# A streaming skewness kernel: eight pooled load buffers against a hand-synchronised ring of two blocks, a loop for the transposes, and part of the row sums on GpSimd

## Chip, cores, metric

One core of one Trainium2 chip. The metric is the device time of one execution in microseconds (us), taken as the median of several executions. A profiled execution also has a span, from the first to the last recorded instruction, which is about 2 us shorter. Each execution has a state: "slow" is more than 1.5% above the fastest execution of the same kernel.

## The reference

```python
x: (1024, 8192) float32                      # setup: standard normal numbers
mean = np.mean(x, axis=-1, keepdims=True)
std  = np.std(x, axis=-1, keepdims=True)
z    = (x - mean) / (std + 1e-8)
return np.mean(z ** 3, axis=-1).astype(np.float32)      # (1024,)
```

The kernels need three sums of each row, of x, of x² and of x³, and close the third moment from them with a few small operations. So 33.55 MB are read once and nearly nothing is written.

## The kernel before

The rows lie as 8 blocks of 128 partitions x 8192 columns. A block is loaded in units (2 to 8 of them), and a unit is cut into slices. ScalarE (ACT) squares a slice and sums x²; VectorE (DVE) multiplies the square by x and sums x³ (the "cube"); TensorE (PE) sums x by transposing all 128x128 tiles of a block into one PSUM tile, which accumulates; ACT copies that tile, and one matrix product with a column of 1/8192 gives the means. GpSimd (POOL) only does small closing operations.

```python
S1_ACT = {(0, 0): 1024, (1, 0): 1024, (2, 0): 1024}   # ACT sums x of 1024 columns of three units
X_BUFS = 8                                            # eight buffers for units, in a pool
SQ_BUFS = 4
...
for k, (w, n_slices) in enumerate(widths):
    last_unit = b == L and k == len(widths) - 1
    xt = xpool.tile([P, w], FP, tag="x", name=f"x_{b}_{k}")
    loads.append(nc.sync.dma_start(out=xt, in_=xv[b, :, c0 : c0 + w]))
    ...
    for s, e in _slices(w, n_slices):
        if last_unit:
            sq = psum1.tile([P, e - s], FP, tag="sqps", name="sqps")     # only here in PSUM
        else:
            sq = sqpool.tile([P, e - s], FP, tag="sq", name=f"sq_{b}_{k}_{s}")
        act(out=sq, in_=xt[:, s:e], func=AF.Square, scale=s_scale, accum_out=s2u[:, j : j + 1])
        cube = ...
        v.scalar_tensor_tensor(out=cube, in0=sq, scalar=1.0, in1=xt[:, s:e],
                               op0=ALU.mult, op1=ALU.mult, accum_out=s3u[:, j : j + 1])
        j += 1
    ...                                               # the ACT sum of S1_ACT
    for c in range((w - w_act) // P):
        nc.tensor.matmul(out=tp, lhsT=xt[:, c * P : (c + 1) * P], rhs=ident,
                         start=(k == 0 and c == 0), stop=(c0 == C and c == n - 1),
                         is_transpose=True)
    for fn in todo.pop((b, k), ()):                   # closings of earlier blocks
        fn()
```

The first six blocks are closed together while the seventh is worked on, the seventh with three GpSimd operations and the rest on ACT while the eighth is worked on, and the eighth at the end. In the final closing the order on each engine is the order of the program.

## Time and profile before

| | before |
|---|---|
| median of 3 executions (range) | 90.77 us (90.76 to 90.84) |
| span of the profiled one, mean granted TensorE clock | 88.8 us, 0.972 |
| first cube starts / last cube ends | 9.96 / 86.13 us |
| tail: from the last cube to the end of the span | 2.7 us |
| sum of the cubes | 73.2 us: 72.3 for 51 in one group of the profile, and the last one, which the profile lists by itself |

The first cube, the last cube and the tail cut the span into an entry, a middle and an end. Two stretches of the time line of the kernel before show the ends of that cut. The columns are start, duration, engine, source line, operation, output<-inputs, shapes, count, and in brackets the idle time of the engine before it and what ended that.

```profile
8.06 1.78 ACT L213 ACTIVATE sq<-x 128x1888 f32<-128x1888 f32 x1 [5.83 <-DMA x<-in_x_dram]
9.96 2.13 DVE L218 SCALAR_TENSOR_TENSOR sq<-sq,x 128x1888 f32<-128x1888 f32 x1 [8.93 <-ACT sq L213]
...
84.50 0.26 ACT L127 COPY tsb<-tp 128x128 f32<-128x128 f32 x1
85.17 0.95 DVE L218 SCALAR_TENSOR_TENSOR cube<-sqps,x 128x768 f32<-128x768 f32 x1
86.36 0.22 DVE L260 SCALAR_TENSOR_TENSOR skew<-sums,t_l,rr_l 128x1 f32<-128x1 f32 x1 [0.22 <-POOL rr_l L259]
```

The first square starts as the first load lands (the landing records: sixteen shares, 7.34 to 7.97 us). At the end the copy of the transposes (84.50) is done before the last cube, so that only one DVE operation and the store come after it. A cube of 1888 columns takes 2.13 us here.

### The profile page before, as it was taken

Reading aid. Unit: us, or ns where it says so; the run is one execution under the profiler, and the core shown is the slowest. Engines: PE = TensorE matmul, PEld = TensorE weight load, DVE = VectorE, ACT = ScalarE, POOL = GpSimd, SP = SyncE. Lnnn points to the kernel's source line nnn. Section 1 sums busy time; section 2 is a strip of 40 time slices with the busy share of each in tenths; the row PEclk is TensorE's granted clock in tenths of the full one; section 3 lists DMA queues with packets and bytes.
Section 4 is the critical chain, followed back from the end, with each engine's and each line's share of the span. In section 5 each row is a group of like instructions: output and inputs, shape, how many; then the busy total and the mean of one; then the engine's idle time right before and its main releaser. Section 6 shows DMA issues by size and latency. Waiting matters only on the chain.

```text
span 88.8 us, 1435 instructions
## 1 busy us (share of the span) xinstructions
PE 64.2 (72%) x504; PEld 58.4 (66%) x504; DVE 73.9 (83%) x110; ACT 74.4 (84%) x137; POOL 13.7 (15%) x18
## 2 busy tenths in 40 slices
PE   0003999492591996989698989497997989897910
PEld 0003999391590995979496889387896868676710
DVE  1000599999799398999999999999999999999980
ACT  6003999699991899999799999499999999999980
POOL 3000000000000000000000000000000079999930
PEclk9999999999999569999999999999999999999996
DMA  4899999999999999999999999999999999997000
GB/s 118 347 420 435 435 413 450 428 420 435 435 420 413 450 413 435 435 420 428 422 424 398 418 425 423 432 420 420 415 410 423 411 406 410 414 412 282 26 0 2
DMA packets 4038, 33.64 MB, mean 379 GB/s; under 512 B 576, under 2 KB 576, under 8 KB 2368
## 3 DMA queue, kind: packets, MB, share of 16 engines
q1 hardware_dynamic: 4032, 33.56, 90.6%
q8 instruction: 4, 0.07, 0.3%
q14 instruction: 2, 0.02, 0.0%
HBM read 33.55 MB, written 0.00 MB: 378 GB/s over the span
## 4 chain that ended last, share of the span: by engine, by line
DMA 55%; DVE 16%; ACT 13%; issue 7%; SPq 4%; POOLq 1%; POOL 0%; ACTq 0%
DMA x<-in_x_dram 55%; DVE sq L218 16%; ACT sq L213 11%; SPq L206 4%; ACT sqps L213 1%; ACT junk L247 1%; POOLq L294 1%; ACT t L190 0%; DVE skew L260 0%; POOL var_l L258 0%; ACT v L187 0%; ACT nm_l L254 0%; ACT tsb L127 0%; ACTq L213 0%; ACT m1sq_l L253 0%
## 5 line engine op out<-in xcount | busy, mean ns | idle before, releaser
L218 DVE SCALAR_TENSOR_TENSOR sq<-sq,x 128x1568 f32<-128x1568 f32 (+20 forms) x51 | 72.3, 1479 | 11.7 <-ACT sq L213 11.5
L213 ACT ACTIVATE sq<-x 128x1568 f32<-128x1568 f32 (+20 forms) x51 | 63.9, 1256 | 11.1 <-DMA x<-in_x_dram 10.5
L231 PE MATMUL tp<-ident,x 128*128 128x128 f32 x488 | 61.9, 286 | 14.5 <-DMA x<-in_x_dram 14.2
L231 PEld LDWEIGHTS tp<-ident,x 128*128 128x128 f32 x488 | 57.0, 148 | 18.2 <-DMA x<-in_x_dram 10.0
L153 POOL TENSOR_TENSOR vara<-m23a,m1sqa 128x6 f32<-128x6 f32 x1 | 2.0, 1975 | 70.3 <-ACT m1sq3a L157 70.3
L213 ACT ACTIVATION_READ_ACCUMULATOR sq<-x 128x1 f32 x51 | 9.5, 187 | 0.0
L130 PEld LDWEIGHTS s1ps<-onesn,tsb 128*128 128x128 f32 x16 | 2.4, 188 | 8.4 <-ACT tsb L127 8.4
L130 PE MATMUL s1ps<-onesn,tsb 128*128 128x1 f32 x16 | 3.1, 260 | 6.5 <-ACT tsb L127 6.5
L218 DVE DVE_READ_ACCUMULATOR sq<-sq,x 128x1 f32 x51 | 4.2, 83 | 0.0
L225 ACT ACTIVATE same<-x 128x1024 f32<-128x1024 f32 x3 | 3.1, 1045 | 0.0
L154 POOL TENSOR_TENSOR rra<-vara,expo 128x6 f32<-128x6 f32 x1 | 2.9, 2874 | 0.1
L127 ACT COPY tsb<-tp 128x128 f32<-128x128 f32 x8 | 2.0, 246 | 0.0
L102 ACT ACT_TABLE_LOAD x1 | 1.3, 1283 | 0.7 <-PEq L283 0.7
L184 POOL TENSOR_TENSOR rr<-var,expo 128x1 f32<-128x1 f32 x1 | 1.4, 1425 | 0.1
L161 POOL TENSOR_TENSOR m23a<-m23a,m1sq3a 128x6 f32<-128x6 f32 x1 | 1.3, 1267 | 0.1
L162 POOL TENSOR_TENSOR skew<-m23a,rra 128x6 f32<-128x6 f32 x1 | 1.2, 1202 | 0.1
L160 POOL TENSOR_TENSOR m1sq3a<-m1sq3a,nm1a 128x6 f32<-128x6 f32 x1 | 1.2, 1200 | 0.1
L183 POOL TENSOR_TENSOR var<-m23m,m1sq 128x1 f32<-128x1 f32 x1 | 1.0, 1043 | 0.0
L218 DVE SCALAR_TENSOR_TENSOR cube<-sqps,x 128x768 f32<-128x768 f32 x1 | 1.0, 955 | 0.0
L196 POOL TENSOR_TENSOR skew<-t,rr 128x1 f32<-128x1 f32 x1 | 0.8, 842 | 0.1
L213 ACT ACTIVATE sqps<-x 128x768 f32<-128x768 f32 x1 | 0.8, 793 | 0.0
L100 DVE MEMSET onesn<- 128x1 f32 x1 | 0.1, 59 | 0.8 <-PEq L283 0.8
(34 smaller groups left out, 7.9 us busy)
## 6 DMA issues: line engine op xcount, KB each, us to landing
x<-in_x_dram SPq DMA_DIRECT2D x8, 2048.0 KB, 23.4
x<-in_x_dram SPq DMA_DIRECT2D x2, 1472.0 KB, 30.2
x<-in_x_dram SPq DMA_DIRECT2D x3, 832.0 KB, 17.9
x<-in_x_dram SPq DMA_DIRECT2D x4, 576.0 KB, 10.6
x<-in_x_dram SPq DMA_DIRECT2D x2, 896.0 KB, 22.9
x<-in_x_dram SPq DMA_DIRECT2D x1, 1728.0 KB, 33.1
x<-in_x_dram SPq DMA_DIRECT2D x1, 1408.0 KB, 25.2
x<-in_x_dram SPq DMA_DIRECT2D x1, 1216.0 KB, 23.2
```

Of the source, the lines that this page charges most:

```text
L102: nc.scalar.activation(out=tiny, in_=onesn, func=AF.Square)
L127: nc.scalar.copy(out=Tsb[b % 2], in_=tps[b])
L130: nc.tensor.matmul(out=s1ps[:, b : b + 1], lhsT=Tsb[b % 2], rhs=onesn, start=True, stop=True)
L153: g.tensor_tensor(out=vara, in0=m2a, in1=m1sqa, op=ALU.subtract)
L154: g.tensor_tensor(out=rra, in0=vara, in1=expo, op=ALU.pow)
L161: g.tensor_tensor(out=m3a, in0=m3a, in1=m1sq3a, op=ALU.add)
L184: g.tensor_tensor(out=mid["rr"], in0=mid["var"], in1=expo[:, 0:1], op=ALU.pow)
L206: loads.append(nc.sync.dma_start(out=xt, in_=xv[b, :, c0 : c0 + w]))
L213: act(out=sq, in_=xt[:, s:e], func=AF.Square, scale=s_scale, accum_out=s2u[:, j : j + 1],)
L218: v.scalar_tensor_tensor(out=cube, in0=sq, scalar=1.0, in1=xt[:, s:e], op0=ALU.mult, op1=ALU.mult, accum_out=s3u[:, j : j + 1],)
L225: act(out=same[:, 0:w_act], in_=xt[:, w - w_act : w], func=AF.Copy, scale=inv_n, accum_out=s1a[:, b : b + 1],)
L231: nc.tensor.matmul(out=tp, lhsT=xt[:, c * P : (c + 1) * P], rhs=ident, start=(k == 0 and c == 0), stop=(c0 == C and c == n - 1), is_transp ...
```

## The change

The intent, as the diff has it: (a) TensorE's instructions run four times as a loop over two blocks, so that its stream is not fetched piece by piece (the trace before has four fetches of 16 KB for 1008 recorded products and weight loads, by division some 250 to a fetch); (b) to get there with 106 transposes for two blocks, GpSimd adds the first 1536 columns of each block to 128 columns, of which TensorE makes one transpose; (c) the pools become a ring of two whole blocks with semaphores set by hand; (d) ACT loses its three sums. The closings move too.

```diff
-S1_ACT = {(0, 0): 1024, (1, 0): 1024, (2, 0): 1024}
 SUB_MAX = 2304
-X_BUFS = 8
-SQ_BUFS = 4
+SQ_BUFS = 5
+S1_POOL = 1536
+RING = 2
 EARLY = 6
+FOLD_PART = 2
+FETCH_SLOT = 0
...
+    ring = sb("ring", RING * C)
+    fold = [sb(f"fold{i}", S1_POOL // 2) for i in range(RING)]
...
+    def first_sum(b):
+        ...
+        f, n = fold[h], S1_POOL // 2
+        tt(("s1p", b), us + free, f, at(b, 0, n), at(b, n, 2 * n), ALU.add)
+        tt(("s1q", b), [("s1p", b)], f[:, 0 : n // 2], f[:, 0 : n // 2], f[:, n // 2 : n], ALU.add)
+        tt(("s1r", b), [("s1q", b)], f[:, 0:P], f[:, 0:P], f[:, P : 2 * P], ALU.add)
+        pr.op("pool", ("s1s", b), [("s1r", b)], lambda: g.tensor_tensor(
+            out=f[:, 0:P], in0=f[:, 0:P], in1=f[:, 2 * P : 3 * P], op=ALU.add
+        ).then_inc(summed, 1), counts=False)
...
+    for u, (b, k, s, e) in enumerate(units):
+        to_pe(u)                                  # ACT tells TensorE that unit u has landed
+        if s < S1_POOL <= e:
+            first_sum(b)
+        ...                                       # squares, cubes, copy of the sums
+        if (b, k) == (F, 1):
+            first_close()                         # six blocks: 6 operations on GpSimd
+        if (b, k) == (L, 2):
+            mid_close()                           # 7th block: 6 operations on GpSimd (3 before)
...
+    for u, (b, k, s, e) in enumerate(units):      # loads: wait for transposes, fold and cubes
+        free = []                                 # of the block two before
+        ...
+        with nc.Fori(0, NB // RING, engines=type(mybir.ALL_ENGINES)([pe_type]),
+                     head_slot={pe_type: FETCH_SLOT}):
+            for h in range(RING):
+                c0 = S1_POOL
+                for i, end in enumerate(PARTS[h]):
+                    tensor.sem_inc(more, -1)._wait_ge(more, 1)
+                    for c in range(c0, end, P):
+                        t = nc.tensor.matmul(out=tp[h], lhsT=at(h, c, c + P), rhs=ident, ...)
+                    ...
+                    if i == FOLD_PART:
+                        tensor.sem_inc(summed, -1)._wait_ge(summed, 1)
+                        nc.tensor.matmul(out=tp[h], lhsT=fold[h][:, 0:P], rhs=ident, ...)
```

The last cube reads its square from SBUF in the changed kernel, as all the others do.

## The prediction

> **What bounds the kernel now.** I read the page of the kernel before first (busy shares, the 40 slices, the queues), then the costliest groups, the waits, the time line of the last 16 us, and last the landing records of the single loads.
>
> ```profile
> PE 64.2 (72%) x504; PEld 58.4 (66%) x504; DVE 73.9 (83%) x110; ACT 74.4 (84%) x137; POOL 13.7 (15%) x18
> ...
> GB/s 118 347 420 435 435 413 450 428 420 435 435 420 413 450 413 435 435 420 428 422 424 398 418 425 423 432 420 420 415 410 423 411 406 410 414 412 282 26 0 2
> ...
> q1 hardware_dynamic: 4032, 33.56, 90.6%
> q8 instruction: 4, 0.07, 0.3%
> ```
>
> The transfers run at 410 to 450 GB/s from slice 3 to slice 36 without a hole: 33.56 MB at about 425 GB/s is 79 us of an 88.8 us span. So loading is the bound, and the rest is about 1.8 us before the first byte and some 6 us after the last (last DVE cube, power, store). Queue q8 is TensorE's instruction fetch: 4 blocks of 16 KB, at 26.9, 47.1, 63.9 and 81.2 us.
>
> ```profile
> L218 DVE SCALAR_TENSOR_TENSOR sq<-sq,x 128x1568 f32<-128x1568 f32 (+20 forms) x51 | 72.3, 1479 | 11.7 <-ACT sq L213 11.5
> L213 ACT ACTIVATE sq<-x 128x1568 f32<-128x1568 f32 (+20 forms) x51 | 63.9, 1256 | 11.1 <-DMA x<-in_x_dram 10.5
> ...
> L153 POOL TENSOR_TENSOR vara<-m23a,m1sqa 128x6 f32<-128x6 f32 x1 | 2.0, 1975 | 70.3 <-ACT m1sq3a L157 70.3
> ```
>
> The second engine is DVE: its 51 cubes take 72.3 us, 9.0 us a block of 8192 columns, against 79/8 = 9.9 us that DMA needs for a block. **DVE has only 0.8 us of slack a block, some 7 us in all.** That is the number on which this case turns.
>
> The time line of the last 16 us shows something else:
>
> ```profile
> 76.81 1.35 DVE L218 SCALAR_TENSOR_TENSOR sq<-sq,x 128x1152 f32<-128x1152 f32 x1
> 77.03 1.20 POOL L160 TENSOR_TENSOR m1sq3a<-m1sq3a,nm1a 128x6 f32<-128x6 f32 x1
> ...
> 78.17 1.35 DVE L218 SCALAR_TENSOR_TENSOR sq<-sq,x 128x1152 f32<-128x1152 f32 x1
> 78.30 1.27 POOL L161 TENSOR_TENSOR m23a<-m23a,m1sq3a 128x6 f32<-128x6 f32 x1
> ...
> 85.48 0.19 POOL L258 TENSOR_TENSOR var_l<-m_l,m1sq_l 128x1 f32<-128x1 f32 x1 [1.19 <-ACT nm_l L254]
> ```
>
> A GpSimd addition of 6 columns takes 1.2 us while a DVE cube runs (77.03 + 1.20 = 78.23, the cube ends at 76.81 + 1.35 = 78.16), and one of a single column only 0.19 us at 85.48, beside the last cube (85.17 to 86.13), the one cube that takes its square from PSUM and so has a single SBUF input. The additions and products of this stage otherwise end 0.05 to 0.07 us after a cube's end: GpSimd waits for DVE. The reverse (DVE waiting for GpSimd) can't be seen here, as 6 columns fit into the 0.08 us between two cubes.
>
> [...]in the landing records each load's sixteen shares come within 0.6 us up to 22 us; from the first fetch on, one of the sixteen comes 1.5 us late for good, from the second another, from the third a third. The last load ends 2.0 us after its first share, not 0.6.
>
> **The change part by part.**
> 1. *TensorE loops.* Its stream of over 1008 instructions becomes 106 transposes (212 load and multiply instructions) plus means and waits[...], run four times. The three fetches inside the loading go. Worth: the spread of the last load falls from 2.0 us to about 1.1 us (two engines also carry a smaller fetch of another engine, the shares at 1.1 and 0.8 us). **About -1.0 us**, if loading stays the bound. [...]its work of 106 x 0.13 us x 4 = 55 us is spread over 75.
> 2. *GpSimd folds 1536 columns a block to 128.* Four additions of 768, 384, 128 and 128 columns = 1408 columns a block, both inputs in SBUF.[...] GpSimd was idle there, so for itself it is free.[...]
> 3. *Ring of two blocks.* 64 KB a partition replace eight buffers of 16 KB. A load waits for cubes, fold and transposes of the block two before. Four loads of 4.9 us go out at the start, the fifth when the first unit is done, some 8 us after it landed, so about 11 us of loads are still queued: no hole by itself. Once DVE lags, the ring makes the loads wait for DVE, and the GB/s of the slices fall.
> 4. *ACT loses three sums of 1024 columns* (3.1 us busy) and gets 27 small semaphore steps. ACT is ahead of DVE afterwards: no effect on the end.
> 5. *Entry.* One more meeting of the engines before the first load: an estimate of +0.3 us, from the 0.4 us that issuing a load takes here.
> 6. *Tail.* From the closing of the first six blocks GpSimd has 6 + 4 + 6 + 2 = 18 operations in order, and gets one at each end of a cube, of which about 12 are left. Some six remain after the last cubes, at 0.2 to 0.5 us; and the last cube now reads its square from SBUF, so the last variance waits for it: **+1 to +2 us**.
>
> Sum with the lock: first square done at 10.1 us (8.06 + 1.78 + 0.3).[...] Before, the span ended 2.7 us after the last cube (86.1 to 88.8), now an estimated 4: span 111, and 1.9 us from span to time as before (90.77 - 88.8): 113. I choose 110, because the hold may be shorter than the whole instruction[...] and some holds fall into waits of DVE in the first two blocks.
>
> **The rivals.**
> - *DVE isn't held up* (the hold is only as long as a short read, or DVE gets its turn between): then loading stays the bound: 90.8 - 1.0 + 0.3 + 1 to 2 = 91 to 92. For it: no cube in the trace before is longer beside a GpSimd operation (1152 columns: 1.35 us each). Against: those read 6 columns. Also for it, as a matter of judgement: a ring, a loop and an unusual fold are effort that one would hardly keep for a loss.
> - *The fetch was the hidden cost and all goes well*, tail included: 89 to 89.8, 1 to 2% faster; over 2% would need 1.8 us, more than the 1.0 us of the spread.
> - *The ring starves DMA*, if a load waits for fold and transposes that come late: +5 us or so without DVE being busier. Against: about 11 us of loads are queued.
> - *Half a hold* (DVE loses half of the GpSimd time)[...].
>
> **Range and chances.** With the lock[...] 107 to 115, with half of it 98 to 103, without it 89 to 93. I give these 65, 18 and 17 in a hundred. Range 97 to 116. Slower by over 2% (above 92.6): 0.84; within 2%: 0.12; faster: 0.04.
>
> **What would show it.** Right: cubes or the gaps between them grow by 3 us a block; DVE busy or waiting for GpSimd to the end;[...] GB/s falling from 430 to about 340 in the middle slices with loads waiting for DVE; queue q8 empty. Wrong: the rate stays at 420 GB/s to slice 36 and DVE's cubes keep their distance of width/0.96 + 0.08 us; or TensorE waits for the fold while DVE is idle (the ring); or a fetch at each loop end.

The sum of this forecast came to 107.1 us for the end of the last cube, so 97.0 from the first cube's start, to 111 us for the span and 113 us for the time, of which 110 was chosen; for the rival of half a hold it came to 100 us. "The lock" in it is an assumption, that a GpSimd addition and a cube with two SBUF operands hold each other up; the trace of the kernel before shows GpSimd's side of it alone (1.20 us for 6 columns beside a cube). The distance of the cubes is taken from that trace: where DVE doesn't wait, they start width x 1.04 ns + 0.08 us after one another (1.27 us for 1152 columns), and each takes width x 1.04 ns + 0.15 us.

## The result

| | before | after | difference |
|---|---|---|---|
| median, 4 executions each | 90.79 us | 117.64 us (116.92 to 118.08) | +26.9 |
| span of the profiled execution | 88.8 | 115.1 | +26.3 |
| first cube starts | 9.96 | 11.46 | +1.5 |
| from the first cube's start to the last cube's end | 76.2 | 94.3 | +18.2 |
| tail | 2.7 | 9.3 | +6.6 |
| sum of the cubes | 73.2 | 94.2 | +21.1 |
| granted clock | 0.972 | 0.866 | |

The changed kernel is correct and slower: the ratio is 1.295 (95% interval 1.288 to 1.302). A ratio is the mean time of one kernel's fast runs over that of the other's of the same rounds, so it is not quite the ratio of the medians. The time lies 1.6 us above the predicted range.

The page of the kernel after, busy times, rate by slice, and TensorE's fetch queue:

```profile
PE 61.7 (54%) x440; PEld 58.2 (51%) x440; DVE 94.8 (82%) x109; ACT 72.0 (63%) x132; POOL 73.5 (64%) x53
...
GB/s 97 387 444 421 433 427 444 421 438 410 444 353 421 376 307 295 362 351 391 181 397 424 422 323 380 310 267 402 379 390 416 156 0 0 0 0 0 3 0 1
...
q8 instruction: 1, 0.02, 0.1%
```

DVE was 83% busy before as well, but now of a longer span: 94.8 us against 73.9. The loads run at the old rate for the first ten slices (a slice is 2.9 us here) and then break off to between 181 and 400 GB/s in places: they no longer set the pace, and the last fifth of the span has no load at all. TensorE fetches one block of instructions (16 KB) where it fetched four. (That queue q8 is TensorE's is borne out by e12, which changes nothing but TensorE's program against e10: the fetch moves from about 4 us, as in e11, to 12.37 us.)

The groups of the kernel after, and the load queue's waits (total, times, longest):

```profile
L232 DVE SCALAR_TENSOR_TENSOR sq<-sq,ring 128x1568 f32<-128x1568 f32 (+21 forms) x52 | 94.2, 1876 | 10.2 <-ACT sq L223 10.2
L238 POOL TENSOR_TENSOR fold<-ring 128x768 f32<-128x768 f32 x8 | 19.7, 2467 | 21.6 <-DMA ring<-in_x_dram 21.6
L248 POOL TENSOR_TENSOR fold<-fold 128x128 f32<-128x128 f32 x8 | 12.6, 1569 | 0.6
```

```profile
SPq L354 <- DVE sq L232: 50.4, 20, 6.2
```

The 10.2 us that DVE waited for ACT lie before its first cube; after it DVE has 0.1 us of gaps in all. All the added time in the middle is therefore **inside** the cubes. GpSimd's additions of 128 columns take 1.6 us on average, nearly as much as one of 768 columns needs alone (1.82 us, below): most of that is waiting. One block of the time line shows how the two engines take turns:

```profile
19.23 2.46 POOL L238 TENSOR_TENSOR fold<-ring 128x768 f32<-128x768 f32 x1 [1.95 <-DMA ring<-in_x_dram]
...
19.94 3.40 DVE L232 SCALAR_TENSOR_TENSOR sq<-sq,ring 128x1568 f32<-128x1568 f32 x1
...
21.78 3.99 POOL L238 TENSOR_TENSOR fold<-fold 128x384 f32<-128x384 f32 x2
...
23.28 2.17 DVE L232 SCALAR_TENSOR_TENSOR sq<-sq,ring 128x1184 f32<-128x1184 f32 x1
...
25.38 1.80 DVE L232 SCALAR_TENSOR_TENSOR sq<-sq,ring 128x1344 f32<-128x1344 f32 x1
25.84 1.66 POOL L248 TENSOR_TENSOR fold<-fold 128x128 f32<-128x128 f32 x1
...
27.11 2.03 DVE L232 SCALAR_TENSOR_TENSOR sq<-sq,ring 128x1568 f32<-128x1568 f32 x1
```

GpSimd starts its 768 columns at 19.23 and has to wait for the cube in progress, which ends at 20.01. It ends at 21.69, 1.68 us after that end; alone it takes 1.82 us. The cube of 1568 columns that wanted to start at 19.94 takes 3.40 us where it takes 1.79 in a quiet place (that its start falls just before the end of the one ahead is nothing special: nearly all cubes of this trace start 0.07 us before it). The next addition then waits behind that cube, and so on: each addition is let in at a cube's end and lengthens the next cube.

| addition | alone | cube beside it | same cube undisturbed | lost by DVE |
|---|---|---|---|---|
| 768 columns | 1.82 us | 1568: 3.40 | 1.79 | 1.61 |
| 384 | 1.00 | 1184: 2.17 | 1.39 | 0.78 |
| 128 | 0.45 | 1344: 1.80 | 1.55 | 0.25 |
| 128 | 0.45 | 1568: 2.03 | 1.79 | 0.24 |

"Alone" is the addition of the first block before any cube (768 and, up to the first cube's start, 384), and for 128 the mean in experiment e3. The sum of the last column is **2.88 us a block**, 2.0 to 2.1 us for every thousand columns that GpSimd adds. Seven blocks lose 20.2 us and the first one, whose 768 columns ran before any cube, about 1.2: 21.4, against 21.1 measured. (The prediction, and the expectation of e1 with its 21.9, left the last cube out of the sum of the kernel before.) All cubes of the changed kernel read two SBUF operands.

The entry of the kernel after:

```profile
9.48 1.78 ACT L223 ACTIVATE sq<-ring 128x1888 f32<-128x1888 f32 x1 [7.08 <-issue]
```

The first square starts 1.4 us later than before. The landing records tell why: fifteen of the sixteen shares of the first load land from 7.57 to 8.35 us, and the last at 9.37. The five loads after it end in the same way, with one share 1.0 to 1.1 us behind the fifteenth. A fetch of TensorE's instructions (16 KB) starts at 3.74 us, inside this load; before, TensorE's first fetch came at 26.9 us.

The end of the kernel after:

```profile
97.53 2.72 POOL L238 TENSOR_TENSOR fold<-ring 128x768 f32<-128x768 f32 x1
...
103.80 1.18 POOL L248 TENSOR_TENSOR fold<-fold 128x128 f32<-128x128 f32 x1
...
105.12 0.45 PE L382 MATMUL tp<-ident,fold 128*128 128x128 f32 x1 [11.25 <-PEq L381]
...
105.36 4.82 PE L374 MATMUL tp<-ident,ring 128*128 128x128 f32 x30
...
110.22 0.27 ACT L256 COPY tsb<-tp 128x128 f32<-128x128 f32 x1 [11.68 <-PE tp L374]
```

The last loads land at 91.6 us, but the fold of the last block starts at 97.53: in GpSimd's order it stands behind the closing of the first six blocks, whose six small operations take from 88.53 to 97.57 us; five of them end 0.06 us after the end of a cube. TensorE waits 11.25 us for the fold, then does its last 30 transposes, the first 14 of them at half the clock: the clock records have 0.5 from 97.9 to 108.2 us, and up to 108.14 the transposes start 0.213 us apart, after it 0.109. The copy that followed the last data by little before now comes 4.4 us after the last cube.

### The profile page after: what moved, and what is told of

It reads as the page before. It is cut to its first block, busy times and chain, and to the rows that moved or that the text cites. A ratio compares the mean times of both kernels' runs of the same rounds, so it can differ in the third digit from the quotient of the medians.

```text
span 115.1 us, 1392 instructions
## 1 busy us (share of the span) xinstructions
PE 61.7 (54%) x440; PEld 58.2 (51%) x440; DVE 94.8 (82%) x109; ACT 72.0 (63%) x132; POOL 73.5 (64%) x53
## 5 line engine op out<-in xcount | busy, mean ns | idle before, releaser
L232 DVE SCALAR_TENSOR_TENSOR sq<-sq,ring 128x1568 f32<-128x1568 f32 (+21 forms) x52 | 94.2, 1876 | 10.2 <-ACT sq L223 10.2
L223 ACT ACTIVATE sq<-ring 128x1568 f32<-128x1568 f32 (+21 forms) x52 | 64.9, 1252 | 24.8 <-DVE sq L232 14.4
L374 PE MATMUL tp<-ident,ring 128*128 128x128 f32 x416 | 58.4, 305 | 12.1 <-PEq L372 11.9
L374 PEld LDWEIGHTS tp<-ident,ring 128*128 128x128 f32 x416 | 54.9, 161 | 13.3 <-issue 13.2
L238 POOL TENSOR_TENSOR fold<-ring 128x768 f32<-128x768 f32 x8 | 19.7, 2467 | 21.6 <-DMA ring<-in_x_dram 21.6
L238 POOL TENSOR_TENSOR fold<-fold 128x384 f32<-128x384 f32 (+1 forms) x16 | 28.9, 1807 | 1.3
L362 PEld LDWEIGHTS s1ps<-onesn,tsb 128*128 128x128 f32 x16 | 3.0, 234 | 21.9 <-issue 21.9
L248 POOL TENSOR_TENSOR fold<-fold 128x128 f32<-128x128 f32 x8 | 12.6, 1569 | 0.6
L382 PE MATMUL tp<-ident,fold 128*128 128x128 f32 x8 | 2.7, 342 | 16.7 <-PEq L381 16.7
L223 ACT ACTIVATION_READ_ACCUMULATOR sq<-ring 128x1 f32 x52 | 9.9, 190 | 0.0
L232 DVE DVE_READ_ACCUMULATOR sq<-sq,ring 128x1 f32 x52 | 4.0, 77 | 0.0
```

The costliest lines, as they stand in the source:

```text
L223: pr.op("act", ("sq", i), waits, lambda: act(out=sqs[i % SQ_BUFS][:, 0 : e - s], in_=at(b, s, e), func=AF.Square, scale=s_scale, accum_out ...
L232: pr.op("dve", ("cube", i), [("sq", i), "sums"], lambda: dve.scalar_tensor_tensor(out=sq, in0=sq, scalar=1.0, in1=at(b, s, e), op0=ALU.mul ...
L238: pr.op("pool", name, waits, lambda: g.tensor_tensor(out=out, in0=in0, in1=in1, op=op))
L248: pr.op("pool", ("s1s", b), [("s1r", b)], lambda: g.tensor_tensor(out=f[:, 0:P], in0=f[:, 0:P], in1=f[:, 2 * P : 3 * P], op=ALU.add).then_ ...
L362: nc.tensor.matmul(out=s1ps[:, h : h + 1], lhsT=tsb[h], rhs=onesn, start=True, stop=True).then_inc(pe, 1)
L374: t = nc.tensor.matmul(out=tp[h], lhsT=at(h, c, c + P), rhs=ident, start=c == S1_POOL, stop=c + P == C, is_transpose=True,)
```

## The experiments

**Theories.** T1 (the "lock" of the prediction and the expectations): DVE and GpSimd hold each other up when both read SBUF operands, and that costs the middle 18 us. T2, its rival: the ring or TensorE's loop slows the cubes. T3: the fold's place in GpSimd's order makes the tail, with the rivals that it is the small operations, or the clock. T4: the jump into TensorE's loop costs 1.4 us at the start. Each "edit" below is against the changed kernel unless it says otherwise.

### e1: no additions (wrong)

```diff
-        tt(("s1p", b), us + free, f, at(b, 0, n), at(b, n, 2 * n), ALU.add)
-        ...                                  # s1q, s1r, s1s
+        pr.op("pool", ("s1p", b), us + free, lambda: g.memset(f[:, 0:1], 0.0))
+        pr.op("pool", ("s1s", b), [("s1p", b)], lambda: g.memset(
+            f[:, 0:P], 0.0).then_inc(summed, 1), counts=False)
```

> The changed kernel without GpSimd's additions: the same ring, loop, waits and signals, but the fold tile is only set to zero (results wrong on purpose). Lock theory (DVE waits while a GpSimd addition reads SBUF): the 21.9 us that the cubes grew by go, DVE busy falls from 94.8 to about 73, loading is the bound again, 90 to 92 us. Ring theory (loads wait for late transposes and fold in a ring of two blocks): the loads still wait for the loop, over 98 us, with slices well under 400 GB/s.

Measured: 93.90 to 96.64 us (four executions, three of them slow, the profiled one too; so no ratio). The time is a **miss**: 90 to 92 was expected. The cubes sum to 73.1 us, as in the kernel before, and end at 88.02, with the ring, the loop and all semaphores in place, and the loads run at 396 to 441 GB/s through the middle. So neither the ring nor the loop slows cubes or loads: T2 falls for the middle. The profile is of a slow execution, so only durations of single operations are taken from it here; e6, whose profile is of a fast one, has the same sum of cubes. The tail stays long (6.5 us): the signal to TensorE still stood behind the first closing, came at 83.1 us, and 30 transposes took 6.20 us.

### e2: the kernel before, plus the additions

```diff
-S1_ACT = {(0, 0): 1024, (1, 0): 1024, (2, 0): 1024}      # edit against the kernel BEFORE
+S1_POOL = 1536
...
+            if skip:                                       # 7 of 8 blocks
+                f = foldp.tile([P, h], FP, tag="fold", name=f"fold_{b}")
+                g.tensor_tensor(out=f, in0=xt[:, 0:h], in1=xt[:, h : 2 * h], op=ALU.add)
+                ...                                        # 384, 128, 128
-            for c in range(n):
+            for c in range(skip, n):
```

> The kernel before with nothing new but GpSimd's four additions, in 7 of the 8 blocks (the last one has no unit wide enough), in place of the sums on ACT; no ring, no loop, the automatic waits of before. Lock theory: the cubes grow by 7 x 2.9 = 20 us, less what the first block hides (1.6) and what fits into 7 us of slack and idle time: DVE's last cube at about 10 + 72.3 + 18.7 = 101, 104 to 108 us. Ring theory: no ring, so 90 to 92 us.

Measured: 106.49 us, ratio 1.174 (1.171 to 1.177), correct; 51 of the cubes 90.6 us (72.3 before), tail 3.1. The groups:

```profile
L215 DVE SCALAR_TENSOR_TENSOR sq<-sq,x 128x1568 f32<-128x1568 f32 (+20 forms) x51 | 90.6, 1840 | 9.2 <-ACT sq L210 9.2
```

The additions alone do it, without ring, loop or hand-set semaphores: cubes +18.3 us for seven blocks. The table of the last section gives 7 x 2.88 less the 1.6 of the first block's 768 = 18.6. T1 stands. With its tail of 3.1 us it also shows that the additions as such don't make a long tail, as long as the last block has none.

### e3: squares in PSUM, so cubes have one SBUF operand

```diff
-SUB_MAX = 2304
-SQ_BUFS = 5
+SUB_MAX = 1024
+SQ_BUFS = 2
-    sqs = [sb(f"sq{i}", SUB_MAX) for i in range(SQ_BUFS)]
+    sqs = [ctx.enter_context(nc.psum_tensor(f"sq{i}", [P, SUB_MAX], FP))[:] for i in range(SQ_BUFS)]
```

(and `_slices` cuts a unit into equal parts of at most 1024 columns.)

> The changed kernel with the squares in PSUM (two buffers of 1024 columns, 72 slices instead of 52, cubes written back in place), so that a cube has one SBUF input; GpSimd adds as in the changed kernel, results right. Lock theory: cubes keep width/0.96 ns + 0.15 us, GpSimd's 768 addition takes 1.8 us everywhere, loading is the bound: 90.5 to 93.5 us. If GpSimd's additions slow DVE or the loads by any other way than DVE's second SBUF input: over 105 us.

Measured: 102.80 us, ratio 1.134 (1.130 to 1.138), correct. The hold is gone, as the time line shows:

```profile
19.27 1.82 POOL L222 TENSOR_TENSOR fold<-ring 128x768 f32<-128x768 f32 x1 [5.83 <-DMA ring<-in_x_dram]
...
19.50 1.23 DVE L216 SCALAR_TENSOR_TENSOR sq<-sq,ring 128x1024 f32<-128x1024 f32 x1
```

The addition takes 1.82 us wherever it falls (mean 1.818 us over all eight, against 2.467), and the cubes beside it 1.23 us like all others of this width. But the time is a **miss**: it did not come down to the loading bound, because this form of the cube costs more of its own. There are 72 slices instead of 52; reading the accumulator takes 0.14 us (result in PSUM) instead of 0.08 (in SBUF); and with two buffers the cubes start alternately 1.18 and 1.32 us after one another, about 1.25 for 1024 columns. Times 64 slices of 1024 columns that is 80 us, more than the 76.2 us that the kernel before takes from its first cube to its last, waits included. DVE also waited 2.2 us (before 34.34) and 1.5 us (before 55.65) for squares, which stood in ACT's order behind a copy that waited for TensorE. The last load landed at 84.4 us (83.5 in the kernel before), the last cube ended at 97.4. DVE stays the bound for another reason. So the run shows the mechanism, but is not a remedy as built.

### e4: the last fold ahead of the first closing

```diff
-        if (b, k) == (F, 1):
+        if (b, k) == (L, 1):
             first_close()
```

> The changed kernel with one line moved: the closing of the first six blocks is put after the last block's fold in GpSimd's order. Queue theory of the tail (the last fold waits behind six small GpSimd operations, so TensorE's last 30 transposes start at 105 us): the last cube stays at about 105.7, the tail of 9.4 us shrinks to 5 to 6.5: 113 to 115 us. If the tail hangs on something else (TensorE's granted clock, the last transposes, ACT's copies): 116.5 to 118 us.

Measured: 113.62 us, ratio 1.254 (1.251 to 1.257), correct: 4.0 us less than the changed kernel from one line, of which the tail accounts for 3.3 (9.3 to 6.0; the cubes end where they did, 105.90). TensorE no longer waits at the end. What is left:

```profile
108.27 0.54 POOL L238 TENSOR_TENSOR rr_l<-var_l,expo 128x1 f32<-128x1 f32 x1
108.96 0.22 DVE L341 SCALAR_TENSOR_TENSOR skew<-sums,t_l,rr_l 128x1 f32<-128x1 f32 x1 [3.05 <-POOL rr_l L238]
```

Now nine small GpSimd operations come after the last cube, from 106.05 on, and end the kernel. Both suspects of T3 are real: first the fold's place, and behind it the queue of small operations.

### e5: no fold at all, TensorE transposes all 64 tiles of a block in its loop

```diff
-S1_POOL = 1536
+S1_POOL = 0
-        if s < S1_POOL <= e:
-            first_sum(b)
...
-                    if i == FOLD_PART:       # and the fold's wait and transpose
```

> The changed kernel with the fold taken out for good: TensorE transposes all 128 tiles of two blocks in its loop[...], GpSimd only closes blocks; results right. If GpSimd (its hold on DVE and its queue in the tail) is the whole loss of the change: 90 to 92 us, with one or two instruction fetches per pass of the loop back in the trace. If the ring and the loop cost something by themselves: 94 us or more.

Measured: 94.10 us median, two executions fast (93.03, 93.76), ratio 1.037 (1.032 to 1.042) as recorded, correct; the two fast executions by themselves lie 2.5 and 3.3% above the kernel before. A **miss**, by 1 to 2 us above what I expected for a kernel without the hold. The cubes are back (72.9 us), loading runs at its old rate, but the first cube starts at 11.72 instead of 9.96, and the tail is 4.1 instead of 2.7. Two blocks were fetched in the whole run, not one or two in each pass as expected, one of them at 4.09 us again.

### e6: write-only operations of the same widths (wrong)

```diff
-        tt(("s1p", b), us + free, f, at(b, 0, n), at(b, n, 2 * n), ALU.add)
-        ...
+        pr.op("pool", ("s1p", b), us + free, lambda: g.memset(f, 0.0))
+        pr.op("pool", ("s1q", b), [("s1p", b)], lambda: g.memset(f[:, 0 : n // 2], 0.0))
+        ...                                  # 128, 128
```

> GpSimd's four additions of the changed kernel become four settings to zero of the same widths, which write SBUF and read nothing (results wrong on purpose). If only GpSimd's reading holds DVE up: cubes as in the kernel before, DVE busy 73 to 75 us, time as with no additions at all, 93 to 97 us. If any GpSimd work of that size holds DVE up: over 100 us, with the cubes longer by the settings' own times.

Measured: 98.39 us, ratio 1.085 (1.077 to 1.092); somewhat above what was expected. The groups:

```profile
L232 DVE SCALAR_TENSOR_TENSOR sq<-sq,ring 128x1568 f32<-128x1568 f32 (+21 forms) x52 | 73.1, 1467 | 14.3 <-ACT sq L223 14.2
...
L245 POOL MEMSET fold<- 128x768 f32 x8 | 5.9, 743 | 53.8 <-DMA ring<-in_x_dram 53.8
```

Cubes of 73.1 us, as against 73.2 in the kernel before: these writes by GpSimd held nothing up. The hold comes from GpSimd's **reading**. Of the 7.4 us that its span is longer than in the kernel before, 4.7 are tail (7.4 us against 2.7): TensorE waited for the signal to 85.3 us and then did 30 transposes in 5.76 us, 22 of them at half clock. 1.8 are the later first cube.

### e7: copies of the same widths, one operand read (wrong)

```diff
-        tt(("s1p", b), us + free, f, at(b, 0, n), at(b, n, 2 * n), ALU.add)
-        ...
+        pr.op("pool", ("s1p", b), us + free, lambda: g.tensor_copy(out=f, in_=at(b, 0, n)))
+        ...                                  # 384, 128, 128
```

(and the loads wait for the third copy, the last that reads the ring.)

> The four additions become four copies of the same widths, with one SBUF input instead of two (results wrong on purpose). If the hold is as long as GpSimd reads: about half of the additions' 2.1 ns a column, so cubes grow by about 0.7 us beside the 768 and by some 1.3 us a block, DVE busy 82 to 86 us, 99 to 107 us in all. If the hold doesn't depend on the number of inputs: as the changed kernel, 116 to 118 us.

Measured: 103.94 us, ratio 1.148 (1.142 to 1.154); DVE busy 80.6 us, a little less than the 82 to 86 that I expected. The groups, and one block of the time line:

```profile
L232 DVE SCALAR_TENSOR_TENSOR sq<-sq,ring 128x1568 f32<-128x1568 f32 (+21 forms) x52 | 80.0, 1601 | 10.3 <-ACT sq L223 10.2
...
L245 POOL COPY fold<-ring 128x768 f32<-128x768 f32 x8 | 11.5, 1438 | 30.7 <-DMA ring<-in_x_dram 30.7
```

```profile
29.04 2.16 POOL L245 COPY fold<-ring 128x768 f32<-128x768 f32 x1 [2.96 <-DMA ring<-in_x_dram]
...
30.44 2.00 DVE L232 SCALAR_TENSOR_TENSOR sq<-sq,ring 128x1184 f32<-128x1184 f32 x1
```

One operand read costs DVE something, and less than half of what two cost: a copy of 768 columns (0.82 us alone) lengthens the cube beside it from 1.39 to 2.00 us, 0.61 against 1.61 for the addition. The same excess, 0.60 to 0.61, stands in six of the seven blocks in which the copy meets a cube; in the other (0.42) DVE came late, as it waited for a square. The copies of 384 columns (0.51 us alone) cost 0.28 to 0.29, those of 128 (0.29 us alone) 0.07 each. So the hold is neither the whole instruction nor a fixed charge for each one. In these records it is GpSimd's own time less 0.21 to 0.22 us, for copies as for additions (1.82 less 1.61, 1.00 less 0.78, 0.45 less 0.24), and a copy costs less because it is done sooner. The settings of e6 don't follow this: they take up to 0.74 us and hold nothing up.

The tail of this run is 10.0 us, by the same way as in the changed kernel: TensorE waits 10.0 us for the last fold, and its last 30 transposes take 5.5 us.

### e8: e1 and e4 together (wrong)

```diff
-        tt(("s1p", b), us + free, f, at(b, 0, n), at(b, n, 2 * n), ALU.add)     # as in e1
+        pr.op("pool", ("s1p", b), us + free, lambda: g.memset(f[:, 0:1], 0.0))
...
-        if (b, k) == (F, 1):
+        if (b, k) == (L, 1):
```

> The run without additions once more, now with the first closing after the last block's signal in GpSimd's order (results wrong on purpose). If its excess over the kernel before came from the late signal and the 30 transposes behind it: 90 to 92 us. If the ring, the loop or the entry cost it: 93 us or more.

Measured: 97.07 us, ratio 1.070 (1.064 to 1.077). A **miss**: I expected 90 to 92. The first load's last share landed at 9.79 us, and the tail was 5.9 us, because a first closing that starts later leaves nine small GpSimd operations after the last cube (to 91.7 us), as in e4. Moving the closing exchanges one end of the queue for the other. It cannot be compared with e1 by time, as e1 was mostly slow.

### e9: e4, with the loop's head at slot 16 of its block

```diff
-FETCH_SLOT = 0
+FETCH_SLOT = 16
```

> The run with the last fold moved ahead, with the loop's head placed at slot 16 of a fetch block instead of slot 0, so that the loop may lie in the block that is loaded already. Theory of the entry (TensorE's jump to a new block fetches 16 KB at 3.7 us and delays one of the sixteen shares of the first loads by 1.2 to 1.5 us, so that the first cube starts at 11.5 instead of 10.0): no fetch at 3 to 5 us, the first load's shares within 0.7 us, first cube at 10.1 to 10.4, time 1 to 1.4 us below the 113.6 us of that run. If the code ahead of the loop doesn't fit into 16 slots: the same fetch, 113.6 us; then the place of the head tells nothing.

Measured: 114.64 us, ratio 1.266 (1.262 to 1.270), against 1.254 for e4 from another call. The fetch was still there, at 3.96 us, which by the expectation would mean that the code ahead of the loop does not fit into 16 slots; the run doesn't show the reason. Inconclusive on T4, as it did not move what it was to move.

### e10: e5, with the seventh block closed as before

```diff
         if (b, k) == (L, 2):
-            mid_close()                  # 6 operations on GpSimd
+            mid_close()                  # variance and power on GpSimd
+        if (b, k) == (L, 4):
+            mid_v3()                     # ACT
+        if (b, k) == (L, 5):
+            mid_t()                      # ACT, then one product on GpSimd
```

(and the reduction of the seventh block's sums moves to the first unit of the last block.)

> The run without any fold (all transposes on TensorE) with the closing of the seventh block as in the kernel before (three small GpSimd operations instead of six, the rest on ACT, spread over the last units). Queue theory of the tail: the four GpSimd operations left at the last cube become one or two, the tail falls from 4.1 to about 2.8 us, 92 to 93 us (that run had 93.0 to 96.1). If the tail doesn't hang on GpSimd's queue: no change.

Measured: 93.72 us, ratio 1.035 (1.032 to 1.037), correct. A **miss** by 0.7 us (92 to 93 was expected). Its profiled execution was slow, so no timings of it are compared, and the closings are read from e11.

### e11: e10, with the loop's head at slot 16

```diff
-FETCH_SLOT = 0
+FETCH_SLOT = 16
```

> The same with the loop's head at slot 16. If the head then lies in the block already loaded, the first loads are not hit by a fetch: first cube at 10.1 to 10.4, one fetch later when TensorE enters its second block, 90.3 to 91.3 us, within 0.6% of the kernel before. If not: as the run before it in this list.

Measured: 93.56 us, ratio 1.032 (1.029 to 1.034), correct. The tail is 3.4 us against 4.1 in e5: three GpSimd operations fewer are worth some tenths, near to what the closing of the kernel before has. The fetch came at 3.91 us all the same and the first cube at 11.54, so this slot tells no more than e9.

### e12: e10, and TensorE waits for the first load before it enters its loop

```diff
     def pe_program(tensor):
         ...
+        tensor.wait_ge(*pr.marks["x", 0])
         with nc.Fori(0, NB // RING, ...):
```

> The run without a fold and with the old closing (head at slot 0), with one wait more: TensorE enters its loop only when the first load has landed. Theory of the entry (the fetch of the loop's block at 3.8 us delays one share of the first load by 1.2 to 1.5 us and with it every cube): the fetch moves to about 8 us, the first load lands by 8.2 us, the first cube starts at 10.1 to 10.4 instead of 11.5, and as DVE has little slack the end moves by 0.8 to 1.4 us: 92 to 92.8 us. If the late first load has another cause (the ring's loads, the extra meeting): first load at 9.3 us and 93.5 us as before.

Measured: 93.71 us, ratio 1.036 (1.032 to 1.041), correct. A **miss** in time: 92 to 92.8 was expected. The time line:

```profile
10.24 2.12 DVE L230 SCALAR_TENSOR_TENSOR sq<-sq,ring 128x1888 f32<-128x1888 f32 x1 [9.00 <-ACT sq L221]
...
14.55 1.19 ACT L221 ACTIVATE sq<-ring 128x1184 f32<-128x1184 f32 x1 [2.40 <-DMA ring<-in_x_dram]
...
15.86 1.39 DVE L230 SCALAR_TENSOR_TENSOR sq<-sq,ring 128x1184 f32<-128x1184 f32 x1 [1.11 <-ACT sq L221]
...
32.93 0.27 ACT L242 COPY tsb<-tp 128x128 f32<-128x128 f32 x1 [2.57 <-PE tp L372]
```

For the first load it is confirmed that the fetch makes it late: the fetch moved to 12.37 us, the last share of the first load landed at 8.15 instead of 9.45 us (e11), and the first cube started at 10.24, 1.3 us earlier than in e11. The jump itself is not confirmed as what sets the fetch off: TensorE's first transpose starts at 8.73, and the fetch, expected at about 8, came 3.6 us after that. And the total did not move. The fetch now fell into the second load: fifteen of its shares had landed by 13.00 us and the last came at 14.43, so that DVE waited 1.11 us for the square before 15.86. In e11 the second load is late too (14.34), but DVE, which began later, has no wait there. So nearly all that the first load gave was lost at the second.

There is also a wait in the middle: the copy of a block's sums stands in ACT's order before the next squares and waited 2.57 us for TensorE, whose clock was 0.5 from 22.6 to 29.4 us; DVE then waited 2.75 us for a square. This is not peculiar to e12: DVE waits 1.61 us at such a copy in e5 (before 33.65) and 3.06 in e11 (before 34.93), each time after a stretch at 0.5. No edit took that wait away, so its worth is not shown. No version that was run beats the kernel before.

### What the runs say together

| | no ring, no loop | ring and loop |
|---|---|---|
| no additions | 90.8 us (before) | 93.4 us (e5, mean of the fast two) |
| additions | 106.5 us (e2, seven blocks) | 117.6 us (after) |

The additions cost 15.7 us without the ring and 24.2 with it. The surplus is mostly the eighth block (2.9 us of hold) and the tail that a fold in the last block brings (9.3 against 4.1 us in e5). The ring and the loop alone cost 2.6 us, or 2.9 to 3.0 in e10 to e12: a longer tail, a later first load and a wait of DVE at ACT's copy, no hole in the loading. In all of these profiles the last load lands between 83.6 and 84.0 us, little later than in the kernel before (83.54). The kernel before had little to gain: its four fetches became one or two. Its own first fetch (26.90 us) cost it a similar sum: the load that follows ended with one share at 29.04, the fifteenth having landed at 27.53, and DVE then waited 1.54 us (before 30.44).

## Why the prediction was right or wrong, by its own steps

The direction (slower, 0.84) and the mechanism held, and the number did not: 117.6 us lies outside 97 to 116.

| step | predicted | measured | difference |
|---|---|---|---|
| first square done, first cube starts (5) | 10.1 us | 11.5 us | +1.4 |
| first cube's start to last cube's end (2) | 97.0 | 94.3 | -2.7 |
| tail (6) | 4 | 9.3 | +5.3 |
| span | 111.1 | 115.1 | +4.0 |
| time by these steps | 113 | 116.9 (this execution) | +4 |
| chosen | 110 | 117.6 (median) | +7.6 |

**Step 6, the tail, is the step that failed: the path that ends the kernel.** It allowed for "+1 to +2 us" from some six small GpSimd operations, and the tail grew by 6.6. It counted GpSimd's small operations but took no account of their order: the last fold stands behind them, TensorE's last 30 transposes behind the fold (11.25 us of waiting), and the copy, the mean and the closing behind those. e4, which moves one line, takes 3.3 us out of the tail. In the changed kernel seven small operations do come after the last cube, as the step said, but five of them are done by 107.5 us, and the transposes end at 110.2: only the other two, which wait for the transposes, are on the path. In e4, with the fold out of the way, the small operations end the kernel, with nine left. Of the 30 transposes 14 started 0.213 us apart and not 0.109, so I estimate 14 x 0.104 = 1.5 us for the clock. What brings the clock down is not shown: in this trace each of TensorE's four longest idle gaps after its first transpose (7.2, 5.2, 3.8 and 11.3 us) has a stretch at 0.5 of 6.8 or 10.2 us that begins 2.5 to 5.1 us after the gap does, and the next longest (2.6 us, from 21.05) has none; but the kernel before has 0.5 from 29.3 to 32.7 us after gaps of 2.5 and 2.0 us (from 20.61 and 27.07), and e8 has it from 33.0 to 39.8 us with no idle gap over 2.5 us ahead of it. No run took the clock away by itself, so its part stays an estimate.

**Step 5, the entry, was too small**: 0.3 us were allowed, and 1.5 came. The prediction noticed in the trace of the kernel before that each fetch delays one of a load's sixteen shares (by 1.4 to 1.5 us after the first fetch), but asked only which fetches go. It listed "a fetch at each loop end" as what would make it wrong, and the one fetch that hurt came at 3.7 us, ahead of the loop's first transpose. e12 shows it: with that fetch out of the way the first cube starts 0.3 us later than in the kernel before, which is what the step allowed for the meeting. As DVE has no gaps after its first cube in the changed kernel, the 1.5 us go into the time in full there; in e12 they don't come back, as the second load is then late.

**Step 2, the hold on DVE, was right in kind and 3.6 us too large.** That DVE is held up was the assumption; the runs show it, with 2.88 us a block, each hold some 0.2 us shorter than the addition takes alone. e1, e2, e3 and e6 each show it from another side: it is the additions, with the ring (cubes of 73.1 us without them, e1) or without it (+18.3 us, e2), only against cubes with two SBUF operands (with one, 1.23 us for 1024 columns, beside an addition or not, e3), and only by GpSimd's reading (73.1 us beside operations that only write, e6). The step had 97.0 us for the middle, of which 72.3 were the cubes; the cubes and the 21.1 us that DVE lost make 93.4, so 3.6 less. That the middle came out only 2.7 us too long is partly luck, as the sum left out the last cube (0.96 us). GpSimd's 768 columns took 1.82 us in the first block and 2.5 on average.

**Step 1, the fetches, was moot.** Three of four went, but the worth of 1.0 us was only to be had if loading stayed the bound. In e5, where loading runs at its old rate, the gain isn't visible: the last load still has a spread of 1.7 us (82.06 to 83.79), as one late share remains from each of two fetches. (The rate of the kernel before lies between 398 and 450 GB/s from slice 3 to slice 36, not 410 to 450; nothing rests on it.)

**Step 3, the ring, was right**: no hole by itself (e1, e5), and once DVE lagged the loads waited for it, 20 waits of 50.4 us in total. **Step 4** was right: ACT's lost sums are nowhere on the path.

**The choice of 110** took 3 us off the sum of the steps because the hold might be shorter than the instruction. The runs give that correction a size, the 3.6 us of step 2, of which 1.0 went to the cube left out. But it was spent on an end of the range where two other terms, each on the path, had been given small values without a check. Without it, 113 and the same width would have held 117.6.

Of the rivals, "DVE isn't held up" is refuted by e2, "the ring starves DMA" by e1 and e5, and "half a hold" by the table of holds; the copies of e7, with one operand read, cost DVE a third (80.0 against 94.2 us of cubes, from 73.2).

Left open: why e1 and e5 spread from 93 to 96 us between executions (perhaps by where the half-clock stretches fall; not shown), what sets off the fetch at 3.7 us, what brings the clock down, what it alone is worth in the tail and at ACT's copies, and whether the 0.2 us by which each hold is shorter than GpSimd's own time belong to the hold or to how the profile takes GpSimd's times.

## What to carry to other kernels

An idle engine is not free when its work holds up the bound engine, as GpSimd's reads of SBUF did here: ask what each instruction given to it takes from the busy one, and price that in the busy engine's time, here 2.0 to 2.1 us for a thousand columns added. When work goes to an engine that takes it in the order of its program, as GpSimd did here (its last fold started at 97.53 us, behind six small operations, though the last load had landed at 91.6), follow that order at the very end of the kernel: what stands behind what, and what waits for the last of it. And before an instruction stream is made to fit, see when its fetches fall and who waits for the late share: here, by the time lines, a fetch cost DVE 1.1 to 1.5 us whether it met the first load, the second (e12) or one in the middle (the kernel before).
